# Sublayer ends of the first transformer block: order of norm, operand and leads, the engine of sums and scalings, split buffers, and pairs of token tiles

## The chip, the core and the metric

The kernel runs on one core of one Trainium2 chip. Five engines work side by side: TensorE (PE; the loading of its stationary operand is listed as PEld), VectorE (DVE), ScalarE (ACT), GpSimd (POOL) and SyncE (SP), which here issues most DMAs. Each takes its instructions in the order in which the compiled program lists them; semaphores tie the engines together. That order is worked out when the kernel is built, by a scheduler that takes the earliest instruction in the program's order that it expects to be ready. The metric is the device time of one execution in microseconds; lower is better.

## What is computed

Two blocks of two layers each. The first block, which the change touches, handles 256 latent and 256 context tokens of width 1024, as four tiles of 128 tokens (0 and 1 latent, 2 and 3 context). All is float32.

```python
def first_block(...):
    h_lat, h_ctx = x, ctx
    for i in range(DEPTH):                       # 2
        m_lat, m_ctx = ...                       # modulation: silu(c) @ w_mod[i] + b_mod[i], 9 vectors each
        h_lat = ffn_sublayer(h_lat, m_lat[0], m_lat[1], m_lat[2], ...)
        h_ctx = ffn_sublayer(h_ctx, m_ctx[0], m_ctx[1], m_ctx[2], ...)
        u_lat = modulate(h_lat, m_lat[3], m_lat[4])
        u_ctx = modulate(h_ctx, m_ctx[3], m_ctx[4])
        y_lat, y_ctx = attention(u_lat, u_ctx)   # layer 0: neighbourhood, layer 1: window (no y_ctx)
        h_lat = layer_norm(ALPHA * h_lat + m_lat[5] * y_lat, ...)
        h_lat = ffn_sublayer(h_lat, m_lat[6], m_lat[7], m_lat[8], ...)
        ...                                      # the same for h_ctx in layer 0
    return h_lat

def ffn_sublayer(h, shift, scale, gate, w_in, w_out, g, b):
    a, v = split(modulate(h, shift, scale) @ w_in)
    return layer_norm(ALPHA * h + FFN_RES * gate * ((silu(a) * v) @ w_out), g, b)
```

So each sublayer ends with a residual and a layer norm over the features, and the next begins with a modulation (multiply by 1 + scale, add shift) of the result. The second block (two layers of mixers and experts on the output) is not touched but for the number of its split buffers, which stays four.

## The kernel before, in words

Every float32 product is made of three matmuls of float32r operands (`mm3`, lines 246 to 249): each operand is split into a high part and the rest. For weights `split` does that (line 460 on ScalarE for the high part, 462 on VectorE for the rest), into four buffers `w0` to `w3` in turn; the raw weights come through six buffers, loaded by SyncE's queue (line 267). For the activations `to_u` does it: TensorE transposes x (line 481), ScalarE applies scale and shift (489), VectorE writes the high part `uh` (493) and the rest `ul` (494), in four rounds of 256 features for a pair of token tiles. The tiles' pairs have column halves of their own in `uh` and `ul`.

A feed-forward (`ffn`) goes in two halves of the hidden width. In each, 11 tiles of input weights give `gh` and `gl` (lines 656 to 661), and then two output products, one for each half `dh` of the features, are accumulated in PSUM by `project`, from six units of two weight tiles (the last of one). `project` runs its first units for all four token tiles in turn, and its last `tail` units token pair by token pair. At the very end (`fh` and `dh` both 1) `tail` is 4, elsewhere 1; with two token tiles it is made 2. Behind each token tile, `residual` scales the product by the gate into the tile `rt` (line 568, VectorE) and adds it to x (570, GpSimd by default, or 572 on VectorE in one operation where x is scaled by ALPHA), and `stats` (587) takes the norm's statistics.

`ln_close` then closes the sublayer: for tiles 0 and 1 it aggregates the statistics (580, 581), takes the root on GpSimd (582), normalises x in place (583) and makes their operand with `to_u`; it returns `rest`, which does the same for tiles 2 and 3 and then multiplies x by the layer norm's rows and adds the other (`ln_finish`, lines 598 and 599, GpSimd), for the residual that comes later. The operand itself has these rows folded into its scale and shift. The next sublayer begins with a lead: the first halves (columns of tiles 0 and 1) of its first products, then `rest()`, then the second halves. In a feed-forward the lead has two weight pairs, in the neighbourhood attention two head pairs, in the window attention four tiles, of which two have a second half. A lead's product takes 24 matmuls of 256 columns per half. There are five such ends in the first block, the last with tiles 0 and 1 alone.

The modulation vectors are computed by VectorE beside all this ("fills", line 383, one weight tile of 512 KB each), doled out by `Pace`, which spreads a number of fills over 57 steps of a feed-forward. `tc.issue_after(ins)` queues instructions behind `ins` on its engine; `tc.high_priority()` puts those of its block ahead of all others that are ready.

Of the kernel before, what the change touches and what calls it, by code (L numbers as in the profile page):

```python
# [199 lines left out]
def build(nc, tc, a, out, es):  # L200
# [3 lines left out]
    def nm(s):  # L204
        uid[0] += 1
        return f"{s}_{uid[0]}"
# [63 lines left out]
    def first_operand():  # L270
        """The first sublayer's operand, a block of 128 features at a time."""
# [76 lines left out]
    fb[0] = pool("fb", first)  # L348
    ccol = const("ccol", fb[0])
# [101 lines left out]
    def split(src, on=V, after=None):  # L451
        shape = list(src.shape[1:])
        n = int(np.prod(shape))
        i = turn["w"] = (turn.get("w", -1) + 1) % 4
        w = dn[0].tile([P, 2, 1024], F32R, tag=f"w{i}", bufs=1, name=nm("w"))
# [56 lines left out]
    def project(units, lhs, toks, evac, tag="A", tail=1, each=None, between=None):  # L512
        """out[t] = sum over k of lhs(k, t).T @ w[k], the last `tail` units tile pair by tile pair."""
# [3 lines left out]
        if tail == 4 and len(toks) == 2:  # L517
            tail = 2
# [45 lines left out]
    def residual(gates, coef, alpha, dh, add=G):  # L564
# [13 lines left out]
    def ln_tile(t, st):  # L578
        mv = per.tile([P, 2], F32, tag="mv", bufs=4, name=nm("mv"))
        V.bn_aggr(mv, st)  # L580
        V.tensor_scalar(mv[:, 1:2], mv[:, 1:2], LN_EPS, None, ALU.add)
        root = G.tensor_tensor(mv[:, 1:2], mv[:, 1:2], halfneg[:, 0:1], ALU.pow)
        norm = V.tensor_scalar(x[t], x[t], mv[:, 0:1], mv[:, 1:2], ALU.subtract, ALU.mult)
        return root, norm
# [16 lines left out]
    def ln_close(l, ln, toks, sts, c_sh):  # L601
        """Normalise the latent tiles and start the next sublayer's operand.

        Returns what does the same for the context tiles and then scales the residual.
        """
# [4 lines left out]
        def part(v):  # L610
            roots = [ln_tile(t, sts[t]) for t in (2 * v, 2 * v + 1)]
            to_u(x, v, sc, sh, uh, ul)
            return roots[-1]

        last = part(0)

        def rest():
            with tc.issue_after((part(1) if len(toks) > 2 else last)[0].ins):
                for t in toks:
                    ln_finish(t, rows)  # L620

        rest.after = last[1]
        return rest

    def ffn(l, j, toks, rest, fills, beside=None):
        pace = Pace(fills, 57)
# [4 lines left out]
        with ExitStack() as st:  # L631
# [4 lines left out]
            for fh in range(2):  # L636
# [53 lines left out]
                elif fh == 0:  # L690
                    lead = []
                    for f in fs[:2]:
                        ws = weights(f, rest.after)
# [4 lines left out]
                    rest()  # L698
                    for f, ws in lead:
# [3 lines left out]
                        finish(f)  # L703
                    fs = fs[2:]
# [9 lines left out]
                for dh in range(2):  # L714
# [4 lines left out]
                    def evac(t, y):  # L719
# [9 lines left out]
                        tail=4 if fh and dh else 1,  # L729
# [6 lines left out]
    with first:  # L736
        first_block(ctx_env)
    second_block(ctx_env)
# [50 lines left out]
def softmax_rows(e, pool, rows, sinks=None, scale=1.0):  # L789
    """rows: (scores in PSUM [128, n], additive bias for the first 256 keys or None).  # L790

    Returns the normalised rows in SBUF.
    """
# [39 lines left out]
def transpose_probs(e, pt, outs, nkb):  # L833
    """Rows of two query tiles to pt [keys, block, 256 queries]."""
# [11 lines left out]
def head_parts(e, pool, src, tag, scale, keys, bufs=1):  # L846
    """Two heads' exact parts, one tile per head.

    Queries: the high part on the head's own rows and the low part on the others.
    Keys: the high part on both, with the low parts of both heads in a tile of their own.  # L850
    """
# [20 lines left out]
def attend_rows(e, pool, q, k, bias, sinks, with_ctx):  # L872
    """Normalised probability rows of two heads on 64 partitions each."""
# [28 lines left out]
def attend_values(e, jobs, v, vcol, o):  # L902
    """Values of two heads into o [128, tokens]."""
# [17 lines left out]
def head_outputs(e, pool, n, last):  # L921
    """Takes the value products of each head pair to the operand of the output product.

    Up to `last` the queries' operand is still read there, so that they wait beside it.
    """
# [19 lines left out]
def neighborhood(e, rest):  # L945
    nc, a, V, S, G, T, nm, per = e.nc, e.a, e.V, e.S, e.G, e.T, e.nm, e.per
    uh, ul = e.uh_ul
    with ExitStack() as st:
# [63 lines left out]
        rest()  # L1012
# [5 lines left out]
        vals[0] = values(0)  # L1018
        score(0)
# [35 lines left out]
def window(e, rest):  # L1055
    nc, a, V, S, G, T, nm, per = e.nc, e.a, e.V, e.S, e.G, e.T, e.nm, e.per
    uh, ul = e.uh_ul
    with ExitStack() as st:
# [64 lines left out]
        rest()  # L1123
# [5 lines left out]
        e.project(e.wunits(a["wav"], KT, 4), lhs, range(4), evac)  # L1129
        for m in range(2):  # L1130
# [12 lines left out]
def rms_scale(e, src, n, dst=None, junk=None):  # L1143
    """1 / sqrt(mean of squares + eps) over the free axis; src [128, n] in SBUF or PSUM."""
# [685 lines left out]
```

## Time and profile before

| | us |
|---|---|
| median of 3 runs | 2681.51 |
| lowest, highest | 2681.08, 2685.47 |
| span of the profiled execution | 2680.9 |
| TensorE busy in it | 2471.9 (92%) |
| VectorE busy | 1686.8 (63%) |
| ScalarE busy | 834.2 (31%) |
| GpSimd busy | 268.7 (10%) |

The profile is one execution, as the hardware profiler took it. Its page has the busy time of each engine, the span in slices, the chain of work that ended last, and the costliest groups of instructions; its other views answer for a stretch: the windows view gives each engine's busy time in it, the number of instructions (x), the granted TensorE clock as a share of 2.4 GHz (PEclk) and the DMA share and rate; the waits view, who waited for whom; the timeline, the instructions in order of time. "L494" is line 494 of the kernel; `ul<-u,uh` is a tile written and those read. Matmuls overlap in the array: their pace is the distance between starts, not the duration.

### The profile page before, as it was taken

Reading aid. Unit: us, or ns where it says so; the run is one execution under the profiler, and the core shown is the slowest. Engines: PE = TensorE matmul, PEld = TensorE weight load, DVE = VectorE, ACT = ScalarE, POOL = GpSimd, SP = SyncE. Lnnn points to the kernel's source line nnn. Section 1 sums busy time; section 2 is a strip of 40 time slices with the busy share of each in tenths; the row PEclk is TensorE's granted clock in tenths of the full one; section 3 lists DMA queues with packets and bytes.
Section 4 is the critical chain, followed back from the end, with each engine's and each line's share of the span. In section 5 each row is a group of like instructions: output and inputs, shape, how many; then the busy total and the mean of one; then the engine's idle time right before and its main releaser. Section 6 shows DMA issues by size and latency. Waiting matters only on the chain.

```text
span 2680.9 us, 33563 instructions
## 1 busy us (share of the span) xinstructions
PE 2471.9 (92%) x12930; PEld 1797.7 (67%) x12930; DVE 1686.8 (63%) x3070; ACT 834.2 (31%) x1412; POOL 268.7 (10%) x215
## 2 busy tenths in 40 slices
PE   7999998999899999899999798999898999888865
PEld 4888877676788888788888666998666422455311
DVE  4977855645798865698886687787654321474211
ACT  3222223656232222222222364445442100343100
POOL 0000013000300000400001501002101010110000
PEclk9999998999999999899999798999999999989977
DMA  8766632222277665266663313887215899646998
GB/s 311 226 196 197 195 102 88 64 79 83 75 223 238 216 229 185 84 222 202 215 200 115 118 32 112 293 294 224 89 62 219 319 402 426 250 137 239 397 426 353
DMA packets 118847, 545.46 MB, mean 203 GB/s; under 512 B 15008, under 2 KB 21408, under 8 KB 106656
## 3 DMA queue, kind: packets, MB, share of 16 engines
q1 hardware_dynamic: 104256, 517.25, 54.9%
q10 hardware_dynamic: 10368, 12.37, 1.6%
q0 software_dynamic: 4064, 13.70, 1.6%
q8 instruction: 102, 1.67, 0.3%
q14 instruction: 57, 0.47, 0.1%
HBM read 542.15 MB, written 1.11 MB: 203 GB/s over the span
## 4 chain that ended last, share of the span: by engine, by line
PE 79%; DVE 8%; DMA 7%; ACT 2%; POOL 2%; issue 2%; ACTq 0%; SPq 0%; POOLq 0%; DVEq 0%
PE pB L249 12%; PE pB L248 12%; PE pB L247 12%; PE pA L247 7%; PE pA L248 7%; PE pA L249 7%; PE pA L1535 5%; DMA big<-in_mgu 4%; PE pB L1581 2%; PE pO L915 2%; PE pT L839 2%; DMA big<-in_mdn 2%; PE pS L880 1%; DVE uh L493 1%; DVE ul L494 1%
## 5 line engine op out<-in xcount | busy, mean ns | idle before, releaser
L248 PE MATMUL pB<-ul,w 128*128 128x512 f32 (+1 forms) x1616 | 581.6, 361 | 12.5 <-DVE ul L494 12.5
L247 PE MATMUL pB<-uh,w 128*128 128x512 f32 (+1 forms) x1616 | 579.2, 361 | 13.6 <-DVE uh L493 11.2
L460 ACT ACTIVATE w<-raw 128x1024 fp32r<-128x1024 f32 (+1 forms) x360 | 372.8, 1037 | 694.4 <-PE pA L249 380.1
L249 PE MATMUL pB<-uh,w 128*128 128x512 f32 (+1 forms) x1616 | 581.6, 360 | 1.2 <-DVE w L462 1.2
L462 DVE TENSOR_TENSOR w<-raw,w 128x1024 fp32r<-128x1024 f32 (+1 forms) x352 | 426.9, 1216 | 204.7 <-ACT w L460 201.5
L383 DVE CUSTOM_DVE_ANT_0 junk<-modw,cb,bmod 128x1024 bf16<-128x1024 f32 x384 | 492.0, 1281 | 9.8 <-DMA modw<-in_wmodd 3.1
L248 PEld LDWEIGHTS pB<-ul,w 128*128 128x128 f32 x1616 | 311.2, 193 | 59.9 <-DVE ul L494 14.5
L247 PEld LDWEIGHTS pB<-uh,w 128*128 128x128 f32 x1616 | 310.1, 193 | 61.4 <-DVE uh L493 13.3
L249 PEld LDWEIGHTS pB<-uh,w 128*128 128x128 f32 x1616 | 311.7, 193 | 48.0 <-issue 4.1
L247 PE MATMUL pA<-w,gh 128*128 128x512 f32 x616 | 242.2, 393 | 2.9 <-DVE rt L568 2.9
L248 PE MATMUL pA<-w,gh 128*128 128x512 f32 x616 | 241.3, 392 | 0.0
L249 PE MATMUL pA<-w,gl 128*128 128x512 f32 x616 | 240.9, 391 | 0.0
L1535 PE MATMUL pA<-big,xs 128*32 128x512 f32 x1536 | 191.7, 640 | 28.6 <-DMA big<-in_mgu 28.6
L248 PE MATMUL pA<-w,uh 128*128 128x512 f32 (+2 forms) x416 | 156.3, 376 | 1.7 <-DVE w L462 1.7
L247 PE MATMUL pA<-w,uh 128*128 128x512 f32 (+2 forms) x416 | 156.7, 378 | 0.0
L249 PE MATMUL pA<-w,ul 128*128 128x512 f32 (+2 forms) x416 | 156.5, 377 | 0.0
L1535 PEld LDWEIGHTS pA<-big,xs 128*32 128x32 f32 x1536 | 48.3, 114 | 155.2 <-issue 104.8
L656 ACT ACTIVATE sa<-pB 128x512 f32<-128x512 f32 (+1 forms) x88 | 48.1, 547 | 288.5 <-PE pB L249 288.5
L247 PEld LDWEIGHTS pA<-w,gh 128*128 128x128 f32 x616 | 115.7, 188 | 30.3 <-DVE rt L568 4.1
L249 PEld LDWEIGHTS pA<-w,gl 128*128 128x128 f32 x616 | 115.7, 188 | 25.6
L248 PEld LDWEIGHTS pA<-w,gh 128*128 128x128 f32 x616 | 115.7, 188 | 24.3
L1581 PE MATMUL pB<-big,hT 128*32 128x512 f32 x768 | 102.2, 628 | 16.6 <-DMA big<-in_mdn 11.6
(302 smaller groups left out, 2964.6 us busy)
## 6 DMA issues: line engine op xcount, KB each, us to landing
big<-in_mgu SPq DMA_DIRECT2D x64, 2048.0 KB, 17.2
modw<-in_wmodd SPq DMA_DIRECT2D x224, 512.0 KB, 4.4
raw<-in_ffin SPq DMA_DIRECT2D x176, 512.0 KB, 4.5
big<-in_mdn SPq DMA_DIRECT2D x30, 2048.0 KB, 17.7
raw<-in_ffout SPq DMA_DIRECT2D x80, 512.0 KB, 4.5
wm<-in_wmodp SPq DMA_DIRECT2D x16, 512.0 KB, 6.0
gate<-gscr POOLq DMA_DIRECT2D x16, 512.0 KB, 6.5
raw<-in_naqk SPq DMA_DIRECT2D x16, 512.0 KB, 3.6
```

The source lines that it names most:

```text
L247: T.matmul(o, lh, rh, start=start, stop=False)
L248: T.matmul(o, lh, rl, start=False, stop=False)
L249: T.matmul(o, ll, rh, start=False, stop=stop)
L383: V.tensor_tensor_reduce(out=junk, in0=w, in1=cb[(b, v)], scale=1.0, scalar=bmod[:, ci, j : j + 1], op0=ALU.mult, op1=ALU.add, accum_out=m ...
L460: S.activation(hi, src, AF.Copy)
L462: sub = on.tensor_tensor(lo, src, hi.bitcast(F32), ALU.subtract)
L493: V.tensor_copy(uh[:, ks, c0:c1], u32)
L656: S.activation(sa[:, :n], pa[:, :n], AF.Silu)
L839: T.transpose(b[:, kb], p[:, kb * P : kb * P + P], e.ident)
L915: T.matmul(o[rs[j], c], v[k0 + kb][:, vcol(j)], pts[j][:, kb], start=kb == 0, stop=kb == nkb - 1, tile_position=(0, 64 * j),)
L1535: T.matmul(pg[v][i][32 * ex : 32 * ex + 32], xs[(v, k // 2)][:, k % 2, c : c + 32], wv[:, ex, i], start=k == 0, stop=k == KT - 1, tile_pos ...
L1581: T.matmul(py[v][32 * ex : 32 * ex + 32], hT[v][:, f, 32 * ex : 32 * ex + 32], wv[:, f2, ex], start=f == 0, stop=f == 3, tile_position=(0, ...
```

## The change

- `ln_close` normalises all token tiles and makes both pairs' operands at once, at high priority, ahead of the next sublayer's lead in the program. `rest` keeps only the scaling by the layer norm's rows, on VectorE.
- `rest()` is called later: in a feed-forward behind the lead's second halves, in the neighbourhood attention behind the first value product, in the window attention behind its value product.
- The sums x + rt (line 570) of the feed-forwards run on VectorE.
- Six split buffers instead of four in the first block; the second block has four as before, counted from the first.
- The last output product of a feed-forward runs all its six units token pair by token pair, with four token tiles. `Pace` has 55 steps, since that product has no head units that call it any more.
- The splits of a feed-forward's lead are no longer queued behind the first pair's norm.

```diff
     def split(src, on=V, after=None):
...
-        i = turn["w"] = (turn.get("w", -1) + 1) % 4
-        w = dn[0].tile([P, 2, 1024], F32R, tag=f"w{i}", bufs=1, name=nm("w"))
+        i = turn["w"] = (turn.get("w", -1) + 1) % n_w[0]
+        w = (dn[0] if i < 4 else fb[0]).tile([P, 2, 1024], F32R, tag=f"w{i}", bufs=1, name=nm("w"))
...
     def project(units, lhs, toks, evac, tag="A", tail=1, each=None, between=None):
...
-        if tail == 4 and len(toks) == 2:
+        if tail >= 4 and len(toks) == 2:
             tail = 2
...
-    def residual(gates, coef, alpha, dh, add=G):
+    def residual(gates, coef, alpha, dh, add=V):
...
     def ln_close(l, ln, toks, sts, c_sh):
...
-        def part(v):
-            roots = [ln_tile(t, sts[t]) for t in (2 * v, 2 * v + 1)]
-            to_u(x, v, sc, sh, uh, ul)
-            return roots[-1]
-
-        last = part(0)
+        with tc.high_priority():
+            for v in range(len(toks) // 2):
+                for t in (2 * v, 2 * v + 1):
+                    ln_tile(t, sts[t])
+                to_u(x, v, sc, sh, uh, ul)
 
         def rest():
-            with tc.issue_after((part(1) if len(toks) > 2 else last)[0].ins):
-                for t in toks:
-                    ln_finish(t, rows)
-
-        rest.after = last[1]
+            for t in toks:
+                ln_finish(t, rows, V)
+
         return rest
 
     def ffn(l, j, toks, rest, fills, beside=None):
-        pace = Pace(fills, 57)
+        pace = Pace(fills, 55)
...
                     for f in fs[:2]:
-                        ws = weights(f, rest.after)
+                        ws = weights(f)
...
-                    rest()
                     for f, ws in lead:
...
                         finish(f)
+                    rest()
...
-                        tail=4 if fh and dh else 1,
+                        tail=6 if fh and dh else 1,
...
@@ neighborhood
-        rest()
         for hp, (ws, bs) in enumerate(lead):
...
         vals[0] = values(0)
+        rest()
         score(0)
...
@@ window
-        rest()
         for m in range(2):
...
         e.project(e.wunits(a["wav"], KT, 4), lhs, range(4), evac)
+        rest()
```

## Rows read from the trace of the kernel before

**Rows 1.** The page, busy time, share of the span and instructions of TensorE.
```profile
PE 2471.9 (92%) x12930; PEld 1797.7 (67%) x12930; DVE 1686.8 (63%) x3070; ACT 834.2 (31%) x1412; POOL 268.7 (10%) x215
```

**Rows 2.** Windows inside a feed-forward: stretch, us, busy by engine, PEclk, DMA share, GB/s.
```profile
751.00:840.00 89.00, 89.00 (x395) 73.71 (x394) 88.03 (x137) 25.74 (x32) 0.00 (x0) 1.00 0.76 236
900.00:1024.00 124.00, 124.00 (x548) 102.64 (x547) 88.65 (x128) 36.71 (x46) 0.00 (x0) 1.00 0.69 227
```

**Rows 3.** Windows, the five sublayer ends: PE, PEld, DVE, ACT, POOL busy.
```profile
399.87:445.67 45.80, 33.81 (x226) 31.93 (x224) 32.23 (x35) 15.46 (x26) 25.90 (x12) 0.81 0.22 75
705.99:749.05 43.06, 33.66 (x226) 31.20 (x225) 32.20 (x36) 14.74 (x24) 22.60 (x12) 0.84 0.21 68
1088.91:1135.05 46.14, 34.10 (x225) 32.21 (x224) 32.12 (x39) 13.57 (x23) 27.00 (x14) 0.82 0.26 83
1475.22:1534.17 58.95, 43.76 (x278) 40.71 (x277) 38.56 (x44) 18.25 (x33) 33.78 (x17) 0.77 0.36 115
1647.12:1677.70 30.58, 19.04 (x113) 17.25 (x113) 26.55 (x32) 10.35 (x16) 12.17 (x6) 0.78 0.28 91
```

**Rows 4.** Timeline of TensorE: start, us, engine, line, operation, tiles, shape.
```profile
399.87 1.03 PE L481 MATMUL pU<-ident,x 128*128 128x128 f32 x8
...
414.63 0.28 PE L247 MATMUL pL<-uh,w 128*128 128x256 f32 x1
414.75 0.28 PE L248 MATMUL pL<-ul,w 128*128 128x256 f32 x1
```

**Rows 5.** Waits of TensorE, 360 to 450 us: total, times, longest.
```profile
PE pL L248 <- DVE ul L494: 6.0, 3, 2.2
PE pL L247 <- DVE uh L493: 4.0, 3, 1.6
...
PE pA L247 <- DVE rt L568: 1.0, 1, 1.0
```

**Rows 6.** Timeline of VectorE at the first end.
```profile
399.99 1.22 DVE L462 TENSOR_TENSOR w<-raw,w 128x1024 fp32r<-128x1024 f32 x1
402.36 0.69 DVE L587 BATCH_NORM_STATS2 st<-x 128x6 f32<-128x512 f32 x1 [1.16 <-POOL x L570]
...
403.56 0.42 DVE L493 CAST uh<-u 128x512 fp32r<-128x512 f32 x1
403.89 2.30 DVE L462 TENSOR_TENSOR w<-raw,w 128x1024 fp32r<-128x1024 f32 x1
...
406.72 0.67 DVE L494 TENSOR_TENSOR ul<-u,uh 128x512 fp32r<-128x512 f32 x1
...
424.93 2.40 DVE L493 CAST uh<-u 128x512 fp32r<-128x512 f32 x1
427.36 2.73 DVE L494 TENSOR_TENSOR ul<-u,uh 128x512 fp32r<-128x512 f32 x1
```

**Rows 7.** Timeline of VectorE at the last end, token tile 1.
```profile
1647.31 0.69 DVE L568 SCALAR_TENSOR_TENSOR rt<-pA,gate 128x512 f32<-128x512 f32 x1
...
1648.80 0.69 DVE L572 SCALAR_TENSOR_TENSOR x<-x,rt 128x512 f32<-128x512 f32 x1
1649.52 0.69 DVE L587 BATCH_NORM_STATS2 st<-x 128x6 f32<-128x512 f32 x1
...
1651.32 0.81 DVE L583 TENSOR_SCALAR x<-x,mv 128x1024 f32<-128x1024 f32 x1 [0.67 <-POOL mv L582]
```

**Rows 8.** Timeline of GpSimd at the first end.
```profile
403.73 1.38 POOL L570 TENSOR_TENSOR x<-x,rt 128x512 f32<-128x512 f32 x1 [1.40 <-DVE rt L568]
408.62 0.78 POOL L582 TENSOR_TENSOR mv<-mv,halfneg 128x1 f32<-128x1 f32 x1 [3.50 <-DVE mv L581]
...
424.13 5.41 POOL L598 TENSOR_TENSOR x<-x,lnr 128x1024 f32<-128x1024 f32 x2 [1.91 <-DVE uh L493]
```

**Rows 9.** Windows, the last 126 matmuls of a feed-forward's last output product.
```profile
370.90:399.87 28.97, 28.97 (x126) 23.72 (x127) 14.28 (x21) 4.88 (x5) 7.84 (x7) 1.00 0.22 64
```

**Rows 10.** Timeline of ScalarE at the first end.
```profile
401.03 1.92 ACT L489 ACTIVATE u<-pU,affh,affs 128x256 f32<-128x256 f32 x4
```

**Rows 11.** Waits of TensorE, 1820 to 1880 us: the second block's operand.
```profile
PE pU L481 <- DVE row L1177: 1.5, 2, 1.3
```

**Rows 12.** Source view of line 570 on VectorE: ns min/median/max, first and last start.
```profile
L570 DVE TENSOR_TENSOR x<-x,rt x12: 680/691/731, 2025.2 to 2462.7; 128x512 f32<-128x512 f32 x12
```

More of the change, by code (lines that the diff above doesn't have):

```diff
@@ L348, in build @@
     fb[0] = pool("fb", first)
+    n_w = [6]
     ccol = const("ccol", fb[0])
@@ L581, in ln_tile @@
         V.tensor_scalar(mv[:, 1:2], mv[:, 1:2], LN_EPS, None, ALU.add)
-        root = G.tensor_tensor(mv[:, 1:2], mv[:, 1:2], halfneg[:, 0:1], ALU.pow)
-        norm = V.tensor_scalar(x[t], x[t], mv[:, 0:1], mv[:, 1:2], ALU.subtract, ALU.mult)
-        return root, norm
+        G.tensor_tensor(mv[:, 1:2], mv[:, 1:2], halfneg[:, 0:1], ALU.pow)
+        V.tensor_scalar(x[t], x[t], mv[:, 0:1], mv[:, 1:2], ALU.subtract, ALU.mult)
     def stats(t, dh, st):
@@ L737, in build @@
         first_block(ctx_env)
+    n_w[0] = 4
+    turn["w"] = -1
     second_block(ctx_env)
```

## The prediction

> **What bounds the kernel now.** Read the page first: TensorE is busy 92% of the span [rows 1], so time can come only from its idle time, from its clock, or from less work for it; the change keeps every matmul. So I next asked the windows view where TensorE is not full. Between the sublayer ends it is: 124.00 us busy of 124.00 and 89.00 of 89.00 in two stretches of the feed-forward sublayer [rows 2]. At the five sublayer ends of the first block it is not, and there the granted clock falls as well: 0.77 to 0.84 instead of 1.00 [rows 3]. A feed-forward end, an attention end, another feed-forward end, the one before the window attention, and the last, with two token tiles, stand there in this order; I call them E1 to E5. Each window runs from the last matmul of the old sublayer to the end of the lead (for E4 to the end of the value product behind it, for E5 to the end of its lead as the spacing of its matmuls gives it).
>
> How long would they last if TensorE never waited and ran at 2.4 GHz? A lead matmul of 256 columns starts 0.12 us after the one before, with the clock at 2.4 GHz; eight transposes take 1.03 us, 0.13 each [rows 4]. E1, E2 and E3 hold 192 such matmuls and 32 transposes: 23.0 + 4.1 = 27.2 us, against 45.80, 43.06 and 46.14, so 18.6, 15.9 and 19.0 are lost. E4 has 48 fewer in its lead and 96 of the value product, 240 in all with 32 transposes and a rotation of 0.5: 33.4 against 58.95, 25.5 lost. E5 has 96 and 16: 13.6 against 30.58, 17.0 lost. That is 96.0. A bank that waits 1.0 us for the scaled product (the tile rt) between the two output halves of E1, E3 and E4 [rows 5] adds 3.0: **99.0 us**, 3.7% of the span, is all that the change can reach at these places.
>
> Which wait ends last there? The waits view names the operand's parts uh and ul, made by VectorE [rows 5]. VectorE's timeline shows why they are late: a weight split of 1.22 is queued ahead of the statistics, these wait for GpSimd's sum (1.16 us idle), and the second pair's parts, 0.42 and 0.67 when alone, take 2.40 and 2.73 [rows 6]. Undisturbed, one tile's scaled product, sum, statistics and norm take 0.69, 0.69, 0.69 and 0.81 [rows 7], and all of it begins only as the old product ends. In those stretches GpSimd multiplies and adds the layer norm's rows over x [rows 8]; parts made outside them take the short time.
>
> **The change, part by part.**
>
> *Six units by pair* (end of the second output half of a feed-forward, four tiles: E1, E3, E4). All 66 matmuls of tiles 0 and 1 run first, then the 66 of tiles 2 and 3. At 28.97 us for 126 matmuls, 0.23 each [rows 9], the second pass lasts 15.2 us instead of 42 x 0.23 = 9.7. No matmul is added. In this pass the first operand can be made. At E2 the last four units are by pair already: 48 x 0.23 = 11.0. At E5 the two tiles go one by one as before.
>
> *Norm and operand ahead of the leads, at high priority.* For a pair: six operations of 0.69, some 0.5 for the aggregates, a GpSimd root of 0.78 [rows 8], two norms of 0.81 [rows 7]: 4.1 + 0.5 + 0.8 + 1.6 = 7 us. Then four rounds of transposes (0.5 each), two ScalarE activations (0.96 a round by the four in 1.92 [rows 10]) and two VectorE parts (1.11): the last part is out 0.5 + 1.0 + 4 x 1.11 = 6 us after the norm, 13 in all, 15.4 with two splits of 1.22 queued between. The second pass plus the 2.1 us of transposes that now stand in it is 17.3 at E1, E3, E4 and 13.1 at E2, where the last round is wanted only 2.2 us into the lead. So the first pair's wait is covered, up to 2 us. The second pair has the same 13 to 15.4 us after the pass; the leads' first halves and its transposes cover 96 x 0.12 + 2.1 = 13.6 us, and the last round is wanted 2.2 us later. Covered too, up to 2 us. If this cover went, each pair would cost what its chain exceeds it by, at most the 13. What is moved past: the transposes now stand among matmuls of the old product and of the lead, and TensorE, which takes them in order, waits if x is late; the matmuls behind them wait along. The same helper, put ahead in this way in the second block, cost 1.5 us at two places [rows 11]; so 0 to 2 us for each of the two insertions, I take 1.5.
>
> *Scalings (the rows of the layer norm) and sums on VectorE.* 36 operations of 128x1024 leave GpSimd, 28 sums of 128x512 too. VectorE has no such scaling yet; its nearest row is the split, two operands in SBUF and the same shape, 1.22 [rows 6]. The sum it has in the second block: 0.69 [rows 12]. So a four-tile end gives VectorE 8 x 1.22 = 9.8 us, a feed-forward 8 x 0.69 = 5.5 more. It gets back what it loses now: in E1 four parts (two stand there, the other two are alike) are over by some 2.0 each, 8 us, and a split of 2.30 by 1.1 [rows 6]. Net 6 us per feed-forward end, 1 at E2. VectorE was busy 32.23 us of E1's 45.80; the shorter end of some 30 us has room for it, since the first pair's share moves into the pass before. What is queued behind the scalings: the next splits. Their cost I take as 0, hidden by two new split buffers, with an upper bound of the whole 9.8 at each four-tile end (2 us more at E4, where rotations and head parts are VectorE's too). At E4 and in E1's attention the scalings stand behind the value product; x is wanted again only at the attention's end, so nobody waits for them but the tables of the scores that reuse their buffers, after a product of over 11 us.
>
> Here a rule speaks against the change. VectorE is busy 88.03 us of 89.00 behind E2 [rows 2], with splits and the modulation fills. The Trainium skill, Perfetto Trace Analysis, section Optimizing Scalar/DVE Operations, says that work may be offloaded from a saturated DVE, even to GPSIMD, and adds that the two share a port, so that it might not help. By its first half the move costs its whole length behind E2 to E4, by the second nothing: the second rival below. With the second half the trace agrees: the cast of 0.42 takes 2.40 while GpSimd scales [rows 6, 8].
>
> *Six split buffers, 55 steps, no queueing of the lead's splits behind the norm.* Buffers of the first units come free at the second pass's start, 2.7 us apart, so the leads' four splits are done before it ends; now the last two run at 399.99 and 403.89, inside E1 [rows 6]. The fills come 57/55 = 3.6% denser, 0.25 us per pair of weight tiles. In the full stretches nothing waits, so 0 there.
>
> **The sum.** What stays of the five losses: E1 and E3 3 each (two insertions of 1.5), E2 4 (shorter cover), E4 7 (3, and 4 for VectorE's extra queue), E5 9: tile 1's chain from 1647.31 to the norm's end at 1652.13 [rows 7] cannot move, transposes, activation and cast make the first lead matmul start at about 1654.3, 6 us lost, and four rounds of 1.11 against 0.72 of matmuls with the clock down cost some 3. The bank's wait goes, 0. That leaves 26 of 99.0: a gain of 73 us. Behind the first block nothing is changed: the second block uses four buffers and its own order; a shift of all its triggers moves it as a whole. 2680.9 - 73 = 2608 for the profiled span. The median of the three runs, 2681.51, is 0.6 above this span: **2609**.
>
> Bounds: with nothing left but E5's 6 the gain is 93 (2588); with insertions at 2 and every chain late by 2 the rest is 45 (2627).
>
> **Rivals.** (1) *The second operand stays behind the lead*, since the compiled order, which is fixed before the chip runs, places its transposes there, as now. For it: VectorE gets x late if the third pair of splits goes first. Against: priority. Then each of four ends keeps a chain of about 5 us (transposes 0.5, activation 1.0, first parts 1.1, three rounds 2.2 with GpSimd out of the way): 2609 + 20 = 2629. (2) *VectorE becomes the bound* behind E2, E3 and E4: splits come late by the 9.8 us that nothing hides: 2609 + 29 = 2638. For it the 99% stretch; against it that those fills run ahead of their need, as the 88.65 us of 124.00 later on show [rows 2]. (3) *Slower: the transposes put ahead block TensorE.* They stand before matmuls that don't need them; if the compiled order takes the chain for short, both pairs' 13 us are paid in the queue, at four ends 104, and E5 keeps its 17: 121 against 99.0, 2680.9 + 22 = 2703. It decides from an average of 12 us per pair. Against it the 1.5 us [rows 11]. (4) *The priority does nothing* to the order that matters and the gains of the sums drown in new queues: within 5 us of 2681.
>
> **Chances.** Forecast (2588 to 2627) 0.68; rival 1 0.12; rival 2 0.11; rival 3 0.04; rival 4 0.05. Faster, that is by over 0.2% or 5.4 us, about what a measurement of this kernel can tell from none, 0.91; same 0.05; slower 0.04. The range must take in rival 1 and rival 2 with a margin: 2588 to 2645.
>
> **What would show it.** Right: at 15 us before each feed-forward end, transposes among the old product's matmuls; the lead begins at once; uh and ul are gone from the waits at E1 to E4; casts of 0.42 throughout; PEclk over 0.95 there; POOL's busy time down by some 130 us (36 x 2.7 and 28 x 1.4 [rows 8]); windows of about 30, 31, 30, 40 and 22 us. Wrong: TensorE waiting for x before transposes (rival 3), for splits w in the stretch behind E2 (rival 2), or for uh behind the lead (rival 1); a VectorE scaling well over 1.22 us would mis-size the third part.

## The result, and the profile after

| | before | after |
|---|---|---|
| median, us | 2681.87 | 2611.76 |
| lowest to highest, 4 runs each | 2681.08 to 2685.47 | 2610.78 to 2612.53 |
| span of the profiled execution | 2680.9 | 2609.0 |

The ratio is 0.9737, with a 95% interval of 0.9723 to 0.9751: the changed kernel is 70 us faster. The forecast was 2609, so its number held. Whether the reasons held is the question of the rest, and most of them did not.

The page's busy times, to be read beside [rows 1]:

```profile
PE 2437.8 (93%) x12930; PEld 1772.0 (68%) x12930; DVE 1677.8 (64%) x3134; ACT 834.6 (32%) x1412; POOL 138.1 (5%) x151
```

GpSimd lost 64 instructions and 130.6 us. VectorE got these 64, and is busy 9.0 us **less** than before. That is the first odd number: 36 scalings of 1.2 us and 28 sums of 0.7 us are 63 us of added work by their lengths.

Next the windows of the changed kernel that answer to [rows 3] (the five sublayer ends E1 to E5; stretch, us, PE, PEld, DVE, ACT, POOL busy, PEclk, DMA share, GB/s). Each begins earlier than its window of before by as much as the instructions ahead of the end do, and ends earlier by as much as those behind it; so the difference in length is what that end gained.

```profile
396.97:424.59 27.62, 26.92 (x218) 25.83 (x216) 24.34 (x35) 11.53 (x18) 3.00 (x2) 1.00 0.29 96
685.10:714.65 29.55, 28.89 (x224) 27.39 (x224) 28.56 (x44) 13.68 (x21) 3.37 (x4) 1.00 0.25 86
1054.50:1082.55 28.05, 27.46 (x216) 26.30 (x215) 27.12 (x41) 10.78 (x16) 3.98 (x4) 1.00 0.37 125
1422.70:1462.37 39.67, 35.27 (x268) 34.26 (x268) 33.01 (x44) 15.47 (x26) 15.84 (x9) 0.96 0.56 176
1575.30:1601.00 25.70, 16.01 (x108) 14.71 (x107) 20.55 (x37) 10.09 (x17) 1.42 (x2) 0.80 0.32 105
```

The gains are 45.80 - 27.62 = 18.2, 43.06 - 29.55 = 13.5, 18.1, 19.3 and 4.9: 73.9 us together. At the first three ends the granted clock is 1.00 where it was 0.81 to 0.84. The rest of the span's 71.9 us lies elsewhere: 2.9 more before E1, and some 5 given back in the second block and at the end, mostly behind 2300 us, in code that the change doesn't touch (both are taken up below).

The waits of TensorE in the changed kernel, from the start to 1860 us (total, times, longest):

```profile
PE pU L482 <- DVE x L584: 12.2, 10, 5.4
...
PE pU L482 <- DVE mv L582: 5.4, 4, 4.4
```

The parts `uh` and `ul` of [rows 5] are gone from it; what is left waits for x and its statistics ahead of transposes, 14.2 of the 17.6 us at E4 and E5. TensorE's timeline of E1 shows why the first three ends are quiet:

```profile
385.11 0.39 PE L248 MATMUL pA<-w,gh 128*128 128x512 f32 x1
385.90 0.66 PE L482 MATMUL pU<-ident,x 128*128 128x128 f32 x4 [0.40 <-DVE x L584]
386.32 0.48 PE L249 MATMUL pA<-w,gl 128*128 128x512 f32 x1
...
398.45 0.40 PE L249 MATMUL pA<-w,gl 128*128 128x512 f32 x1
398.68 0.28 PE L247 MATMUL pL<-uh,w 128*128 128x256 f32 x1
```

The transposes of the first pair stand amid the old product, 13 us before its end, and cost 0.40 us of waiting; the lead's first matmul follows the last old one without a gap. In [rows 4] these transposes came behind the old product.

### The profile page after: what moved, and what is told of

Its sections match the earlier page's. It is cut to its first block, busy times and chain, and to the rows that moved or that the text cites. A ratio compares the mean times of both kernels' runs of the same rounds, so it can differ in the third digit from the quotient of the medians.

```text
span 2609.0 us, 33471 instructions
## 1 busy us (share of the span) xinstructions
PE 2437.8 (93%) x12930; PEld 1772.0 (68%) x12930; DVE 1677.8 (64%) x3134; ACT 834.6 (32%) x1412; POOL 138.1 (5%) x151
## 4 chain that ended last, share of the span: by engine, by line
PE 80%; DMA 7%; DVE 7%; ACT 2%; POOL 2%; issue 2%; ACTq 0%; SPq 0%; POOLq 0%; DVEq 0%
PE pB L247 12%; PE pB L248 12%; PE pB L249 12%; PE pA L249 7%; PE pA L247 7%; PE pA L248 7%; PE pA L1534 5%; DMA big<-in_mgu 3%; DMA big<-in_mdn 3%; PE pB L1580 2%; PE pO L914 2%; PE pT L838 2%; PE pS L879 1%; PE pS L878 1%; PE pX L1781 1%
## 5 line engine op out<-in xcount | busy, mean ns | idle before, releaser
L247 PE MATMUL pB<-uh,w 128*128 128x512 f32 (+1 forms) x1616 | 573.6, 357 | 2.0 <-DVE hp L867 1.4
L249 PE MATMUL pB<-uh,w 128*128 128x512 f32 (+1 forms) x1616 | 575.2, 356 | 0.2 <-DVE w L463 0.2
L463 DVE TENSOR_TENSOR w<-raw,w 128x1024 fp32r<-128x1024 f32 (+1 forms) x352 | 421.5, 1200 | 208.0 <-ACT w L461 207.5
L247 PEld LDWEIGHTS pB<-uh,w 128*128 128x128 f32 x1616 | 305.2, 189 | 49.0 <-issue 1.8
L249 PEld LDWEIGHTS pB<-uh,w 128*128 128x128 f32 x1616 | 305.5, 189 | 47.5 <-issue 3.5
L248 PEld LDWEIGHTS pB<-ul,w 128*128 128x128 f32 x1616 | 305.7, 189 | 45.3 <-issue 2.7
```

The costliest lines, as they stand in the source:

```text
L247: T.matmul(o, lh, rh, start=start, stop=False)
L248: T.matmul(o, lh, rl, start=False, stop=False)
L249: T.matmul(o, ll, rh, start=False, stop=stop)
L463: sub = on.tensor_tensor(lo, src, hi.bitcast(F32), ALU.subtract)
```

## The experiments

Two theories stood against each other. By mine, the **order** (norm and operand ahead of the lead, at high priority, covered by a longer second pass) brings the larger part and VectorE's new work next to nothing by itself. By the rival, the **engine** does it: GpSimd's sums and scalings lengthen the VectorE operations that they run beside, and the order hardly matters. All times below are medians; the kernel before, run beside each of them on the same chip, had 2683.0 to 2683.2 us.

### Engine or order

*Vector only*: the kernel before, with scalings and sums on VectorE and its order as it was, but that the scalings are no longer queued behind the second pair's root (`issue_after`).

```diff
-    def residual(gates, coef, alpha, dh, add=G):
+    def residual(gates, coef, alpha, dh, add=V):
...
-            with tc.issue_after((part(1) if len(toks) > 2 else last)[0].ins):
+            if len(toks) > 2:
+                part(1)
+            with ExitStack():
                 for t in toks:
-                    ln_finish(t, rows)
+                    ln_finish(t, rows, V)
```

> The kernel before, with the scalings by the layer norm's rows and the sums x + rt on VectorE; order, buffers and pairs as before. Theory (the order hides the operands, the engine only lets VectorE run undisturbed): the chains still begin when the old product ends, so TensorE still waits there; only the slowed parts (four of some 2 us in each four-tile end) and GpSimd's sums go. Gain some 5 us per end, 20 to 30 us in all: 2652 to 2662. Rival A (GpSimd beside VectorE is the cause of the waits, the order adds little): 60 us or more, below 2622. Rival B (VectorE has no room for 9.8 us of scalings per end): no gain or slower, 2680 and up.

Measured: 2612.99 us, ratio 0.9739 (0.9722 to 0.9755). That is the whole gain, with nothing of the new order. The window of this kernel that answers to E1:

```profile
399.97:430.80 30.83, 28.13 (x215) 26.96 (x216) 26.55 (x41) 12.04 (x24) 2.23 (x2) 0.94 0.16 56
```

30.83 us, 15.0 less than before, though here the transposes still stand behind the old product and those of the second pair behind the lead. Matched instructions (the same matmul, by its number, in both profiles) give 15.0, 12.6, 14.7, 19.1 and 9.1 us for the five ends, 70.5 together. VectorE's timeline at E1 in this kernel says how:

```profile
404.04 0.42 DVE L493 CAST uh<-u 128x512 fp32r<-128x512 f32 x1
404.37 1.22 DVE L462 TENSOR_TENSOR w<-raw,w 128x1024 fp32r<-128x1024 f32 x1
...
423.49 0.42 DVE L493 CAST uh<-u 128x512 fp32r<-128x512 f32 x1
423.82 1.22 DVE L598 TENSOR_TENSOR x<-x,lnr 128x1024 f32<-128x1024 f32 x1
424.96 0.69 DVE L494 TENSOR_TENSOR ul<-u,uh 128x512 fp32r<-128x512 f32 x1
```

At E1 a cast takes 0.42, the rest 0.69 and a split 1.22 throughout, where [rows 6] has 2.40, 2.73 and 2.30. A scaling of 1.22 now stands between the parts, and a cast followed by a scaling and a rest, 2.3 us, is still less than one lengthened cast.

*GpSimd kept*: the changed kernel with scalings and sums back on GpSimd.

```diff
-    def residual(gates, coef, alpha, dh, add=V):
+    def residual(gates, coef, alpha, dh, add=G):
...
-                ln_finish(t, rows, V)
+                ln_finish(t, rows, G)
```

> The kernel after, with the scalings and the sums back on GpSimd; order, priority, buffers and pairs as after. Theory: the operands are still made under the old product and the lead, but the scalings of tiles 0 and 1 now run on GpSimd just while the second pair's chain needs VectorE, whose casts of 0.42 then take about 2.4 again, and the GpSimd sums (1.3 to 2.2) and roots stand in the chain: some 5 to 8 us back per end, 25 to 40 of the 70 lost: 2637 to 2652. Rival A (the engine is the main part): 2660 and up. Rival C (the order alone is all of it): within 5 us of 2612.

Measured: 2693.03 us, ratio 1.0040 (1.0026 to 1.0053): slower than before. The order alone doesn't bring 30 to 45 us, it loses 10. GpSimd's timeline at E1 of this kernel, then VectorE's, then TensorE's:

```profile
395.51 5.23 POOL L598 TENSOR_TENSOR x<-x,lnr 128x1024 f32<-128x1024 f32 x2 [3.91 <-PE pU L482]
```

```profile
395.11 0.42 DVE L494 CAST uh<-u 128x512 fp32r<-128x512 f32 x1
395.56 2.90 DVE L495 TENSOR_TENSOR ul<-u,uh 128x512 fp32r<-128x512 f32 x1
398.39 2.64 DVE L494 CAST uh<-u 128x512 fp32r<-128x512 f32 x1
```

```profile
418.52 1.12 PE L482 MATMUL pU<-ident,x 128*128 128x128 f32 x4 [6.95 <-DVE x L584]
419.29 0.56 PE L249 MATMUL pL<-uh,w 128*128 128x256 f32 x1
```

The cast at 395.11, ahead of the first scaling, takes 0.42 us; the rest and the cast behind it, 0.69 and 0.42 alone, are longer by 2.2 each, while GpSimd's scalings take 2.6 each. The norm of the second pair comes late, and the transposes that the new order has put into the lead stop TensorE for 6.95 us, with lead matmuls queued behind them. This is the mechanism of the prediction's third rival. GpSimd's work sets it off, since the changed kernel differs in nothing else; whether by the lengthened operations or by its slow sums in the chain, this run doesn't tell.

*Scalings only* and *sums only* on VectorE, in the kernel before: the first has the second part of the edit of vector only, the second its first line.

> The kernel before, with the scalings by the layer norm's rows on VectorE; the sums stay on GpSimd. New theory (the earlier one, that the order is the main part, has fallen): a VectorE operation that meets a GpSimd scaling ends only when that one ends, so 94 us of scalings hold up VectorE's parts just where TensorE waits for them; moved, they free most of it: 45 to 60 us of the 70, 2623 to 2638. Rival (the sums in front of the statistics are the cause): 2660 and up.

> The kernel before, with the sums x + rt on VectorE; the scalings stay on GpSimd. New theory: a sum of 1.4 to 2.2 on GpSimd becomes 0.7 in the chain of each tile behind the three feed-forward ends, and the wait of 1.0 us for the bank goes: 8 to 20 us, 2663 to 2675. Rival (the sums are the cause): below 2640.

Measured: 2625.74 us (ratio 0.9783, 0.9769 to 0.9798) and 2666.92 us (0.9935, 0.9918 to 0.9951). The scalings are worth 57.2 us and the sums 16.1, 73.3 together, against 70.1 for both at once.

### Contention, or the wait for x

Moving the scalings changes two things: GpSimd no longer works beside VectorE, and x is ready at another time. *Idle GpSimd* takes vector only and has GpSimd compute as many products of 128x1024 as it did before, at the same places, from the two layer-norm rows into a tile that nobody reads. It keeps the queueing by `issue_after`, which vector only dropped; VectorE's operations at E1 come in the same order in both.

```diff
                 for t in toks:
-                    ln_finish(t, rows)
+                    ln_finish(t, rows, V)
+                for _ in range(2 * len(toks)):
+                    idle = fb[0].tile([P, D], F32, tag="idle", bufs=1, name=nm("idle"))
+                    G.tensor_tensor(idle, rows[0], rows[1], ALU.mult)
```

> The kernel before with scalings and sums on VectorE, as in the run with VectorE alone, and beside it as many GpSimd products of 128x1024 as there were scalings, at the same places, from two tiles that stay to one that nobody reads. The extra products are work left to no purpose; the outputs are untouched. New theory (what costs is GpSimd's and VectorE's sharing of the way to SBUF, not that anybody waits for GpSimd's results): VectorE's casts take about 2.4 again and most of the gain goes, 2650 to 2690. Rival F (the gain came from results that arrive sooner, or from a shorter GpSimd queue for the roots): within 6 us of 2613.

Measured: 2687.08 us, ratio 1.0016 (1.0004 to 1.0027). VectorE has the scalings here as in vector only, and x is ready no later for GpSimd's sake; still, work that nothing waits for takes away all 70 us and a little more. GpSimd's and VectorE's timelines of this kernel at E1:

```profile
408.66 22.84 POOL L623 TENSOR_TENSOR idle<-lnr,lnr 128x1024 f32<-128x1024 f32 x8
```

```profile
408.72 2.88 DVE L583 TENSOR_SCALAR x<-x,mv 128x1024 f32<-128x1024 f32 x1 [0.44 <-POOL mv L582]
411.53 3.42 DVE L599 TENSOR_TENSOR x<-x,lnr 128x1024 f32<-128x1024 f32 x1
...
421.44 2.56 DVE L493 CAST uh<-u 128x512 fp32r<-128x512 f32 x1
424.04 2.73 DVE L494 TENSOR_TENSOR ul<-u,uh 128x512 fp32r<-128x512 f32 x1
```

Eight products in 22.84 us are 2.86 each. In the same stretch VectorE gets through about one operation per product: a norm of 0.81 takes 2.88, a scaling of 1.22 takes 3.42, a cast of 0.42 takes 2.56, a rest of 0.69 takes 2.73. Each is longer by 2.0 to 2.2, whatever its length alone. A shared bandwidth would stretch the long ones more; these durations look like a turn that is waited for.

### The parts of the order

*Tail of four*: the changed kernel with the last four units by pair, as before, and 57 steps. *No priority*: the changed kernel without `high_priority` in `ln_close`.

```diff
-                        tail=6 if fh and dh else 1,
+                        tail=4 if fh and dh else 1,
...
-    pace = Pace(fills, 55)
+    pace = Pace(fills, 57)
```

> The kernel after, with the last four units by pair as before (the second pass has 42 matmuls, 9.7 us, instead of 66, 15.2 us), 57 steps, still six buffers. Theory: the first pair's chain of 13 us and two splits does not quite fit under 9.7 + 2.1 us: 1 to 4 us per feed-forward end, three of them: 2615 to 2624. Rival D (the longer pass is what hides the operand): 5.5 us each, 2628 or more.

```diff
-        with tc.high_priority():
+        with ExitStack():
             for v in range(len(toks) // 2):
```

> The kernel after, with norm and operands at the same place in the program but without high priority. Theory: the first pair's transposes fall behind the old product's matmuls, which are ready earlier and stand earlier in the program, so their chain (transposes 0.5, activation 1.0, parts 1.1 a round) is bare again: 6 to 9 us per four-tile end, some 30 in all, 2636 to 2648; the second pair's still come ahead of the lead where x is ready. Rival E (the place in the program alone does it): within 5 us of 2612.

Measured: 2608.57 us (ratio 0.9731, 0.9715 to 0.9746) and 2614.64 us (0.9748, 0.9733 to 0.9762). Neither is told apart from the changed kernel: the 3 to 12 us that I gave the pairing and the 24 to 36 for the priority were wrong. By matched matmuls the profile without priority loses 2.4 and 2.3 us at E1 and E3, too little for these runs to show.

*Evacuation first*: the changed kernel with the last output half's residual and statistics at high priority too, meant for the waits that were left at E4 and E5.

```diff
                     def evac(t, y):
-                        res(t, y)
-                        if fh == 1:
-                            stats(t, dh, sts[t])
+                        with tc.high_priority() if fh and dh else ExitStack():
+                            res(t, y)
+                            if fh == 1:
+                                stats(t, dh, sts[t])
```

The attention's evacuation was edited alike.

> The kernel after, with the scaled product, the sum and the statistics of each sublayer's last output half at high priority too. Two ends still wait for the norm there: 4.4 us before the window attention and 5.4 and 3.6 us at the last end, where splits of 1.2 and fills of 1.3 stand between statistics, aggregate and norm on VectorE. Theory: these go ahead, and 5 to 9 us of the 14 come back: 2603 to 2607. Rival (the order on VectorE there is set by what is ready, not by priority): within 3 us of 2612.

Measured: 2611.52 us, ratio 0.9732 (0.9717 to 0.9747): no gain, and the wait of 4.4 us at E4 is still there. What makes it is shown under "What was left at E4 and E5".

*Six buffers*: the kernel before with six split buffers and nothing else.

```diff
-        i = turn["w"] = (turn.get("w", -1) + 1) % 4
+        i = turn["w"] = (turn.get("w", -1) + 1) % n_w[0]
```

> The kernel before with six split buffers instead of four in the first block and nothing else. Theory: the first sublayer gains the 2.9 us that the changed kernel was ahead by its end, and the sublayer ends keep their losses, since GpSimd's work still lengthens VectorE's: 2677 to 2682. Rival (the buffers are what let the leads' splits leave the end): the splits at 399.99 and 403.89 go ahead and each of the four-tile ends gains 2 to 4 us: 2665 to 2676.

Measured: 2705.25 us, ratio 1.0084 (1.0067 to 1.0101): 22 us slower, which neither theory had. By matched matmuls E2 and E3 lose 7.7 and 7.1 us, E5 another 3.6. VectorE's and TensorE's timelines of this kernel at E2:

```profile
721.10 3.43 DVE L384 CUSTOM_DVE_ANT_0 junk<-modw,cb,bmod 128x1024 bf16<-128x1024 f32 x1
...
724.57 3.25 DVE L384 CUSTOM_DVE_ANT_0 junk<-modw,cb,bmod 128x1024 bf16<-128x1024 f32 x1
...
733.69 0.42 DVE L494 CAST uh<-u 128x512 fp32r<-128x512 f32 x1
```

```profile
734.17 1.01 PE L247 MATMUL pB<-uh,w 128*128 128x256 f32 x3 [7.77 <-DVE uh L494]
```

With more buffers the splits run ahead, and the modulation fills come out of the order sooner: several now stand between the norm and the first cast, and beside GpSimd's scalings a fill of 1.28 takes 3.25 to 3.43. A cast that came at 723.66 in the kernel before comes at 733.69. The 2.9 us that the changed kernel is ahead before E1 are not the buffers' either: this kernel has none of them there, and sums only, with four buffers, has the same 2.9. They look like a difference between executions: nearly all of it arises in the first 50 us, and there idle GpSimd, with its matmuls in the order of the kernel before, is 2.3 us ahead of that kernel, and evacuation first, in the order of the changed one, 2.0 behind it.

### What was left at E4 and E5

In the changed kernel GpSimd still makes six splits of the window attention's weights. Its timeline at E4, VectorE's beside it, and the wait that follows on TensorE:

```profile
1429.99 3.03 POOL L463 TENSOR_TENSOR w<-raw,w 128x1024 fp32r<-128x1024 f32 x1 [17.26 <-ACT w L461]
...
1434.47 2.34 POOL L463 TENSOR_TENSOR w<-raw,w 128x1024 fp32r<-128x1024 f32 x1
```

```profile
1430.84 3.25 DVE L463 TENSOR_TENSOR w<-raw,w 128x1024 fp32r<-128x1024 f32 x1
1434.54 2.82 DVE L584 TENSOR_SCALAR x<-x,mv 128x1024 f32<-128x1024 f32 x1 [0.44 <-POOL mv L583]
```

```profile
1437.41 0.65 PE L482 MATMUL pU<-ident,x 128*128 128x128 f32 x4 [4.40 <-DVE mv L582]
```

It is the same meeting of the two engines, a split and a norm lengthened by 2.0 each. *Window splits* moves these six to VectorE in the changed kernel; *order kept, window splits* does so in vector only.

```diff
         def tile_weights(m):
-            on = G if m >= 4 else V
-            return e.split(e.raw(...), on)
+            return e.split(e.raw(...))
```

> The changed kernel, with the six weight splits of the window attention that still ran on GpSimd (128x1024, two inputs) put on VectorE. Theory (a two-input GpSimd operation lengthens the VectorE operation that it meets): the stall of 4.4 us at E4, where a VectorE split took 3.26 us and a norm 2.82 beside GpSimd's splits of 3.03 and 2.34, goes down to under 1 us; 2605 to 2610, that is 2 to 6 us under the changed kernel's 2611.8. Rival (VectorE's load): six more splits of 1.22 us make 7.3 us that VectorE has to find in E4 and in the window attention; then 2612 to 2619, and the stall at E4 is at least as long.

> The kernel before, with scalings and sums on VectorE and its own order, and the window attention's six splits on VectorE as well: nothing of the new order, priority, pairing or buffers. Theory (engines are everything, order next to nothing): as the order-kept kernel, 2613.0, less what the window splits cost it, 1 to 4 us: 2608 to 2612, within 4 us of the changed kernel with the same splits on VectorE. Rival (order matters once GpSimd is out of the way): at least 6 us slower than that kernel, 2613 or more.

Measured: **2597.61 us** (ratio 0.9687, 0.9668 to 0.9705) and 2607.12 us (0.9722, 0.9702 to 0.9742). The first beats both kernels, by 85.6 us the one before and by 14.2 the changed one. Its window of E4, and the same two VectorE operations:

```profile
1422.70:1455.70 33.00, 32.31 (x255) 30.97 (x254) 30.17 (x49) 15.21 (x25) 3.97 (x4) 1.00 0.65 210
```

```profile
1430.60 1.18 DVE L463 TENSOR_TENSOR w<-raw,w 128x1024 fp32r<-128x1024 f32 x1
1432.21 0.81 DVE L584 TENSOR_SCALAR x<-x,mv 128x1024 f32<-128x1024 f32 x1 [0.44 <-POOL mv L583]
```

E4 is 39.67 - 33.00 = 6.7 us shorter. By matched matmuls the window attention behind it gains 1.0 more and E5 0.4: some 8 us, more than the 2 to 6 expected; the clock at E4, 0.96 before, comes back to 1.00 too. About 5 us more lie far behind, in the attention of the second block's second layer, whose code is the same in both. The windows of that stretch, first of the changed kernel, then of window splits:

```profile
2310.00:2372.00 62.00, 58.22 (x225) 36.61 (x224) 34.94 (x118) 23.74 (x52) 4.88 (x7) 0.92 0.32 111
```

```profile
2302.65:2359.70 57.05, 53.28 (x225) 34.22 (x224) 35.07 (x118) 23.40 (x52) 4.87 (x7) 1.00 0.35 121
```

The same 225 matmuls take 5 us more with the granted clock at 0.92. This is also most of what the changed kernel gave back behind 2300 us. But it isn't shown to be the window splits' doing: by matched matmuls this stretch takes 57.2, 58.7 or 62.1 us in each of the fourteen profiles, and which of them doesn't follow order or engine. The kernel before has 58.7, scalings only, in the old order, the 62.1 of the changed kernel, and GpSimd kept and six buffers the 57.2 of window splits. Why was not found, nor whether a kernel has the same in every execution: a profile is one.

Order kept is 9.5 us behind window splits, and its highest and lowest runs (2604.5 to 2612.8) don't meet those (2596.4 to 2599.9). So my expectation of within 4 us was wrong: once GpSimd is out of the way, the new order as a whole is worth something. How much is less sure. Of the 12.8 us between the two profiled executions, matched matmuls put 5.8 between the start of E1 and the end of E5, 4.7 before E1, where executions differ anyway, and 2.3 behind. Over vector only the order was worth 1 us by the medians. One difference is at E4 with the attention behind it, where matched matmuls give the order 0.2 us with the window splits on GpSimd and 3.8 without.

*Window splits, old order at E5*: as window splits, but with two token tiles no priority and the lead's splits queued behind the norm.

```diff
-        with tc.high_priority():
+        with tc.high_priority() if len(toks) > 2 else ExitStack():
...
+        rest.after = norm if len(toks) == 2 else None
...
-                        ws = weights(f)
+                        ws = weights(f, rest.after)
```

> The changed kernel with the window splits on VectorE, and at the end with two token tiles (E5) the order of the kernel before: no high priority, and the lead's splits queued behind the norm. Theory: at E5 the changed kernel waits 5.39 and 3.62 us because weight splits and modulation fills stand in VectorE's queue between the statistics and the norm; the order-kept kernel gained 9 us there, the changed one 4.9, so this gives 4 us more than the window splits alone: 2600 to 2606. Rival (the waits at E5 are the chain's own, and the fills are queued there in any order): as the window splits alone, 2605 to 2610.

Measured: 2599.40 us, ratio 0.9690 (0.9671 to 0.9710): no gain. VectorE's timeline at E5 of this kernel:

```profile
1573.15 0.69 DVE L587 BATCH_NORM_STATS2 st<-x 128x6 f32<-128x512 f32 x1
1573.75 1.27 DVE L384 CUSTOM_DVE_ANT_0 junk<-modw,cb,bmod 128x1024 bf16<-128x1024 f32 x1
...
1575.07 1.28 DVE L384 CUSTOM_DVE_ANT_0 junk<-modw,cb,bmod 128x1024 bf16<-128x1024 f32 x1
...
1577.16 0.81 DVE L584 TENSOR_SCALAR x<-x,mv 128x1024 f32<-128x1024 f32 x1 [0.73 <-POOL mv L583]
```

Two fills of 1.28 us still stand between the last tile's statistics and its norm, which starts 4.0 us after them, as in the changed kernel. The traces show where the fills come from: in all eight kernels with six split buffers one or two fills stand there, in all six with four buffers none, and *six buffers* differs from the kernel before in nothing else. In vector only, with four, the norm starts 1.8 us after the statistics, and E5 gains 9.1 us instead of 4.9. The changed kernel with four buffers was not run, so what E5 would gain in it is open.

## Why the prediction was right in number and wrong in reason

*What bounds the kernel now* held. The 99.0 us of loss were the right place to look: 73.9 came back there, and 25.1 stayed, against 26 forecast. That the total agrees so well with the wrong share for order and engines is luck: the move of engines alone gains 70.1 us, and the order, which was to bring most, costs 10.0 alone. Most of the signs that the prediction named came true, but they didn't tell the two apart: in vector only, too, casts take 0.42 at E1, and the waits for `uh` and `ul` of lines 493 and 494 in the first block are down from 48.0 to 3.0 us. By end (E1, E3 and E4 with a bank's wait of 1.0 each, which is gone) 1.4, 2.4, 1.9, 7.2 and 12.1 us stayed, against 3, 4, 3, 7 and 9.

*The step that failed* is the one that says which part of the change brings this. The prediction read two causes from [rows 5 to 8]: the chain begins too late, and parts in it are lengthened beside GpSimd. It gave the first nearly everything, in "covered" waits of 13 to 15.4 us per pair, and booked the second as 8 to 9 us of work that VectorE gets back, with "net 6 us per feed-forward end" of work added. The term was mis-sized, because the lengthened operations are not work beside the chain, they are the chain. VectorE's timeline at E1 in the kernel before has three more of them than [rows 6]:

```profile
412.36 2.89 DVE L583 TENSOR_SCALAR x<-x,mv 128x1024 f32<-128x1024 f32 x1 [0.44 <-POOL mv L582]
...
430.01 2.58 DVE L493 CAST uh<-u 128x512 fp32r<-128x512 f32 x1
432.63 2.72 DVE L494 TENSOR_TENSOR ul<-u,uh 128x512 fp32r<-128x512 f32 x1
```

A norm that takes 0.81 alone, and two of the four rounds of parts, 0.42 + 0.69 alone, are longer by 2.0 to 2.2 per operation, 10.3 us in five operations. Scalings only gains 10.2 us at E1 by matched matmuls: there the lengthening comes back about whole as TensorE's time, which the prediction had taken for VectorE's alone. Measured, the scalings are worth 57.2 us and the sums 16.1; the order without them costs 10.0.

*Six units by pair*: the cover of 15.2 instead of 9.7 us wasn't needed; 2608.57 without it. *Norm and operand ahead, at high priority*: insertions of 1.5 us each were forecast; at E1 the waits ahead of transposes are 0.8 and 0.3 us in all. Without priority the kernel is 2.9 us slower, inside the two intervals. The order as a whole brought 3.2, 0.9, 3.4, 0.2 and -4.2 us at the five ends over vector only, 3.5 together. *Scalings at 1.22* and *sums at 0.69* were priced rightly: their medians in the changed kernel are 1218 and 684 ns. *Six buffers at 0* was wrong for this part alone, 22 us slower; inside the whole change it isn't 0 at E5 either, where the buffers bring the fills ahead of the norm, but the change was not run with four buffers. *E4 at 7* came out right for another reason than its VectorE queue: it was GpSimd's window splits, which the prediction didn't see, though [rows 3] has GpSimd busy 33.78 us there, more than at any other end. *E5 at 9* was 3 too low: two fills stand in the last tile's chain, which the old order with four buffers doesn't have there.

*The rivals.* Rival 1 (the second operand behind the lead) is part of what vector only does, and its price of 5 us per end was too high: with the first operand late too, vector only loses 3.2, 0.9, 3.4 and 0.2 to the changed kernel there. Rival 2 (VectorE becomes the bound) fell: VectorE has 64 instructions more and is busy 9 us less, and up to 1860 us TensorE waits 0.2 us in all for a split that VectorE makes. Rival 3's mechanism is real, but its large waits at the four-tile ends come with GpSimd's work left in place: 6.95 us in one insertion in GpSimd kept, 4.40 at E4 beside the window splits. Rival 4, that the priority does nothing, was near the truth for the priority itself; what it overlooked, as I did, is that the sums and scalings carry the gain.

The Trainium skill, SBUF — State Buffer, section SBUF: two separate sides, has the port pair that VectorE and GpSimd share as "an exclusive lock, not a bandwidth split": whoever starts first, GpSimd or a VectorE operation with two inputs in SBUF or in a two-port mode, holds it for the whole instruction. The trace agrees, with casts of 0.42 that take 2.40 to 2.64, about one per GpSimd operation; which mode the casts and norms ran in, no run here shows. The prediction used the Trainium skill's Perfetto Trace Analysis, section Optimizing Scalar/DVE Operations, only to ask whether VectorE would get too much work; it should have asked how many operations of the critical chain meet a GpSimd operation, and what each of them then lasts.

## What to carry to other kernels

Where a chain on VectorE is waited for, look at GpSimd's timeline beside it before anything else: here each VectorE operation of these kinds that met a GpSimd product of 128x1024 became some 2 us longer, and a cast of 0.42 loses as much by it as a split of 1.22. Such work can be cheaper on VectorE even if VectorE already looks like the busier engine: 63 us of moved work left it 9 us less busy and the kernel 70 us faster. And a gain that a sum assigns to several parts should be split by running each part alone: here the part that was booked at a few microseconds carried nearly all of it, and the one that the sum was built on cost time by itself and was worth something only once GpSimd was out of the way.

## What the runs showed of the hardware

- A GpSimd product of 128x1024 that no one needs slows VectorE as much as one that matters: eight of 2.86 us in a row let through about eight VectorE operations, each 2.6 to 3.4 us long, that is 2.0 to 2.2 longer than alone.
- It goes both ways: GpSimd's sum of 128x512, 1.38 in [rows 8], took 2.17 and 2.24 us in GpSimd kept, where a split on VectorE had begun 0.2 us or less before it.
- TensorE's granted clock is part of the price of a wait. At E1 to E3 it went from 0.81 to 0.84 up to 1.00 as the waits went, and in the second block the same 225 matmuls took 57.05 us at 1.00 and 62.00 at 0.92.
